# A hybrid flow step on one core: order of the output pairs' loads, spread-out weight sums and squares, and a last pair in pieces

## The chip, the cores and the metric

The kernel runs on one NeuronCore of a Trainium2 chip. Its engines are TensorE (PE in the profile; its weight loads are PEld), VectorE (DVE), ScalarE (ACT), GpSimd (POOL) and SyncE (SP), which here only issues DMAs. Each engine works through its own list of instructions in order and waits where an instruction needs something that another engine or a DMA has not finished. The metric is the time of one execution on the device, in microseconds. Before the change three runs took 2201.45, 2194.2 and 2185.36 us, so the median is 2194.2 us.

## What is computed

The reference is one layer of a backbone for 128 prompt tokens and 2048 sample tokens with 1024 channels. Both groups go through the same steps, which make 2176 token rows in all:

```python
xn = rmsnorm(h, ln_g) * (1.0 + scale) + shift
proj = einsum('btd,de->bte', xn, w_in)           # 1024 -> 7696 columns
o_a = delta_bidir(...)                            # gated DeltaNet scan, forward and backward
o_b = chunk_sgu(...);  o_c = fourier_mix(...)     # spatial gating, Fourier mixing
br = stack([o_a, o_b, o_c])                       # each 512 wide, times its SiLU gate
pb = einsum('btnw,nwd->btnd', br, w_branch)
merged = einsum('btnd,btnd->btd', sigmoid(gates), pb)
h = h + gate * einsum('btd,de->bte', merged, w_out)
y = rmsnorm(h, final_g)
```

The change touches the part from `pb` on: the merge of the three branches, the product with `w_out` and the last norm.

## The kernel before

Every fp32 product is made from float16 halves: each operand is written as a high and a low half (`halves`, or `converting` for weights: ACT writes the scaled high half, DVE the rest), and a product is three matmuls (high·high, high·low, low·high). The scale of the halves comes from a sum of squares, which ACT makes with an accumulating Square.

The work stands in stages. After the input projections, the DeltaNet scan runs piece by piece beside the spatial gating, the Fourier mixing and the first two merges (`pace.tick` starts the next piece). `merge(n, ...)` is called for the branches 1, 2 and 0 in this order. Each call goes over 8 blocks of 128 output channels (`db`), and in each over five tiles of tokens, four of 512 and one of 128. For a tile TensorE makes the gate's product (24 matmuls, or 8 x 3) and the branch's (12, or 4 x 3) into two of the three banks of PSUM named `ps_mm`; ACT makes the sigmoid of the first (L1711), DVE multiplies the second with it (L1720), POOL adds the result to the running sum `mrow` (L1721). A bank comes free when ACT or DVE has read it, so TensorE can be ahead of them by about one tile.

Beside this main line, other work is put in:

- In `merge(2)`, `finish_delta` (called at the start of each block) loads a block of the third branch's weights and sums its squares on ACT (L1764 to L1766), eight in all.
- In `merge(0)`, `tail` calls `out_w(db)` for the first four blocks. It prepares two of the eight column blocks of `w_out`: loads, two squares (L1803), two high and two low halves of 1024 elements (L1792 and L1793, called at L1810), and then four differences of weight quarters, made on POOL (L1814), split into halves and written to DRAM (`tD`).
- In `merge(0)` from the fifth block on, `quarters` makes from two blocks of merged values seven operands for a tile (sums and differences on DVE and POOL, then halves of 512, 256 and 1024 elements a partition) and writes them to DRAM (`paD`, L1833).
- `gate_rows` makes the adaLN gate in steps (L464 and L466 on DVE).

The output stage is `one_tile(16)` for the 128 prompt rows, then eight pairs of 128-row tiles. A pair takes seven products of 12 matmuls 512 wide in place of eight (Strassen's scheme on the 2 x 2 blocks of rows and of `w_out`): `two_tiles`. It needs the operands of the pair from DRAM (`next_pair`, L1896: 128 partitions x 14 KB, 1792 KB), the summed weights `tw` (L1906: four loads of 1 MB into the place of `xl`), the gate row `gb` (L1901) and the last norm's row `fg` (L1907), each 512 KB.

The operands lie in three buffers. One is in the pool `orp`; as `desk` the same bytes are the work place of `out_w` and `quarters` until the last L1833 has read them. Two are in the pool `op`, which opens in the place of `big` (`mrow` and the branch values `o16`) once `merge(0)` is over. Here pairs 0, 3 and 6 are loaded into the `orp` buffer, the others into `op`.

No list of times fixes the order. The kernel's scheduler orders the instructions of each engine, and so the DMAs on SP's queue, from the order of the source, from `high_priority` blocks and from `issue_after`, which puts an instruction behind a named one.

## Time and profile before

| | us |
|---|---|
| median of three runs | 2194.2 |
| the profiled execution, by its own clock of time | 2185.07 |
| its span from first to last instruction | 2183.3 |
| TensorE busy in the span | 2086.8 (96%) |
| VectorE, ScalarE, GpSimd busy | 1357.1, 1056.4, 765.5 |
| DMA moved | 403.36 MB, 185 GB/s on average |

The profiled execution was the fastest of the four that were timed; 1.8 us of its time lie outside the span. In a row of the profile, the number before the engine is the start or the busy time; the square bracket behind a row gives how long the engine stood idle before it and what ended the wait. The columns of a table by windows are busy time by engine with the number of instructions, then the clock that TensorE was granted (1.00 is full speed), the busy share of the DMA engines and what they moved.

### The profile page before, as it was taken

What the parts mean: (1) busy time and instruction counts of PE and PEld (TensorE: products, weight loads), DVE (VectorE), ACT (ScalarE), POOL (GpSimd) and SP (SyncE); (2) the same over time, 40 slices, a digit from 0 to 9 for tenths busy, and PEclk for the clock granted to TensorE, in tenths of its full rate; (3) what the DMA queues carried; (4) which work ended last, traced back from release to release, by engine and by line L of the source; (5) the groups of instructions that cost most, each with busy time, mean ns of one, the idle gap of its engine ahead of it and who ended that gap; (6) DMA issues with size and microseconds to landing.
All of it is one profiled execution on the core that took longest, in us unless ns stands there. A gap on an engine that the chain in (4) does not pass through costs nothing. (4 is left out here: it accounts for less than half of the span.)

```text
span 2183.3 us, 42589 instructions
## 1 busy us (share of the span) xinstructions
PE 2086.8 (96%) x16122; PEld 1193.9 (55%) x16122; DVE 1357.1 (62%) x3070; ACT 1056.4 (48%) x2428; POOL 765.5 (35%) x939
## 2 busy tenths in 40 slices
PE   7999999999899999999899999899999999997997
PEld 4455444465455677786555655456555444443443
DVE  6657754389879797466655546655564665565244
ACT  5544744466555664444644446655553433343111
POOL 0321432233434332444122223344533244334355
PEclk9999999999999999999999999999999999999999
DMA  9526631277776743444755456866654644457562
GB/s 351 217 71 203 250 125 71 95 239 217 240 231 210 234 140 95 128 142 129 225 165 167 153 170 205 255 203 200 209 187 152 203 161 166 161 186 295 193 236 111
DMA packets 222925, 403.36 MB, mean 185 GB/s; under 512 B 39720, under 2 KB 109888, under 8 KB 219904
## 3 DMA queue, kind: packets, MB, share of 16 engines
q1 hardware_dynamic: 167648, 290.98, 41.8%
q0 software_dynamic: 15248, 65.95, 8.3%
q10 hardware_dynamic: 39824, 43.72, 6.0%
q8 instruction: 126, 2.06, 0.4%
q14 instruction: 79, 0.65, 0.1%
HBM read 258.26 MB, written 142.30 MB: 183 GB/s over the span
## 5 line engine op out<-in xcount | busy, mean ns | idle before, releaser
L241 PE MATMUL b<-xh,whi 128*128 128x512 f16 (+1 forms) x1920 | 650.9, 348 | 8.4 <-DVE sg L1720 5.5
L241 PE MATMUL b<-xl,whi 128*128 128x512 f16 (+1 forms) x1920 | 651.1, 348 | 0.0
L241 PE MATMUL b<-xh,wlo 128*128 128x512 f16 (+1 forms) x1920 | 650.3, 348 | 0.0
L241 PEld LDWEIGHTS <-whi 128*128 128x128 f16 x3872 | 353.0, 98 | 329.9 <-issue 14.5
L241 PEld LDWEIGHTS <-wlo 128*128 128x128 f16 x1936 | 189.4, 98 | 176.4 <-issue 2.1
L241 PE MATMUL b<-big,bhi 128*128 128x512 f16 (+1 forms) x960 | 250.8, 348 | 3.8 <-ACT big L1677 2.6
L241 PE MATMUL b<-big,blo 128*128 128x512 f16 (+1 forms) x480 | 163.1, 347 | 0.2 <-DVE blo L318 0.2
L1721 POOL TENSOR_TENSOR mrow<-mrow,sg 128x512 f32<-128x512 f32 (+1 forms) x80 | 99.2, 1242 | 153.0 <-DVE sg L1720 119.3
L241 PEld LDWEIGHTS <-xh 128*128 128x128 f16 x1496 | 119.4, 99 | 32.5 <-issue 3.2
L943 POOL TENSOR_TENSOR cy<-cy,raw 128x545 f32<-128x545 f32 (+1 forms) x48 | 65.9, 1399 | 182.9 <-ACT raw L942 182.9
L241 PEld LDWEIGHTS <-bhi 128*128 128x128 f16 x960 | 86.1, 98 | 79.3 <-issue 4.0
L241 PEld LDWEIGHTS <-pa 128*128 128x128 f16 x684 | 66.9, 99 | 98.3 <-issue 20.7
L1711 ACT ACTIVATE sg<-b,winv 128x512 f32<-128x512 f32 (+1 forms) x120 | 73.8, 615 | 65.2 <-PE b L241 64.6
L241 PE MATMUL b<-whi,xh 128*128 128x128 f16 x544 | 96.1, 223 | 2.7 <-DVE yT L1629 1.9
L241 PE MATMUL b<-whi,xl 128*128 128x128 f16 x544 | 96.1, 223 | 0.0
L241 PE MATMUL b<-wlo,xh 128*128 128x128 f16 x544 | 96.1, 223 | 0.0
L1177 POOL COPY T<-ES 32x256 f16<-32x256 f16 x68 | 27.5, 404 | 191.6 <-DMA ES<-ei 172.8
L1720 DVE SCALAR_TENSOR_TENSOR sg<-b,binv,sg 128x512 f32<-128x512 f32 (+1 forms) x80 | 53.2, 666 | 62.1 <-PE b L241 55.4
L318 DVE SCALAR_TENSOR_TENSOR wlo<-wst,wsc,whi 128x1024 f16<-128x1024 f32 x52 | 68.9, 1327 | 33.3 <-ACT whi L317 33.3
L305 ACT ACTIVATE wlo<-wst 128x1024 f16<-128x1024 f32 x52 | 55.0, 1058 | 70.1 <-DMA wst<-in_w_blk_dram 65.2
L241 PE MATMUL b<-xl,pa 128*128 128x512 f16 x384 | 86.7, 379 | 1.6 <-DVE st L1967 1.6
L241 PEld LDWEIGHTS <-xl 128*128 128x128 f16 x816 | 74.6, 99 | 13.4
(506 smaller groups left out, 4256.2 us busy)
## 6 DMA issues: line engine op xcount, KB each, us to landing
wst<-in_w_blk_dram SPq DMA_DIRECT2D x58, 512.0 KB, 4.9
pa<-pa POOLq DMA_DIRECT2D x16, 896.0 KB, 4.1
pa<-pa SPq DMA_DIRECT2D x8, 1792.0 KB, 8.0
qkv<-cy POOLq DMA_DIRECT2D x12, 1089.0 KB, 5.3
st<-br SPq DMA_DIRECT2D x48, 256.0 KB, 3.6
mrow<-mrg SPq DMA_DIRECT2D x16, 576.0 KB, 3.9
dc<-dec SPq DMA_DIRECT2D x17, 512.0 KB, 4.2
kq<-qkv SPq DMA_DIRECT2D x34, 256.0 KB, 4.8
```

Of the source, the lines that this page charges most:

```text
L241: newest[0] = PE.matmul(out, l, r, start=start, stop=stop, skip_group_check=reopened)
L305: w.squared = A.activation(w.lo, st, AF.Square, accum_out=ss)
L318: w.low = V.scalar_tensor_tensor(w.lo, st, s, w.hi, ALU.mult, ALU.subtract)
L943: G.tensor_tensor(y[:, c0:c1], y[:, c0:c1], raw[:, 1 + c0:1 + c1], ALU.mult)
L1177: G.tensor_copy(T16[rows(a0, b), :, :, b], ES[0:32, :, 2 * a0 + b, :, wT])
L1711: A.activation(sg, ps, AF.Sigmoid, scale=gw.inv)
L1720: V.scalar_tensor_tensor(sg, ps, binv[:, 1:2], sg, ALU.mult, ALU.mult)
L1721: G.tensor_tensor(mr, mr, sg, ALU.add)
```

## The change

1. **Pairs' buffers and loads.** Pairs 2 and 5 now use the buffer in `orp`; pairs 0, 1, 3, 4, 6 and 7 use those in `op`. In the source the first pair's load stands behind the loads of `tw` 1 and 2, ahead of `gb`, of `tw` 0 and 3 and of `fg`.
2. **Squares of the third branch's weights.** They leave `finish_delta`; `norm_step` makes one after each tile from the third block of `merge(2)` on, behind that tile's sigmoid.
3. **`out_w` in steps.** It becomes a generator. `merge` calls `out_step` after each tile, which takes two steps. The halves of 1024 elements become two of 512, and each square stands behind a sigmoid.
4. **`quarters`.** The last halves, 1024 elements a partition, become two of 512.
5. **The last pair.** Its end goes by pieces for both tiles, as the last part of the diff shows.

```diff
     def finish_delta(db):
-        st = sb(ep, [P, 512], "st", bufs=3)
-        SY.dma_start(st, w_brb[0, db])
-        A.activation(st, st, AF.Square, accum_out=bsums[:, 3 + db:4 + db])
         if db == KT - 1:
             pace.drain()
+    early = list(range(KT))
+    def norm_step(db):
+        if db > 1 and early:
+            i = early.pop(0)
+            st = sb(ep, [P, 512], "st", bufs=3)
+            SY.dma_start(st, w_brb[0, i])
+            with tc.issue_after(gated_[0].ins):
+                A.activation(st, st, AF.Square, accum_out=bsums[:, 3 + i:4 + i])
-    inv_ = merge(2, False, inv_, finish_delta, then=(0, 17))
+    inv_ = merge(2, False, inv_, finish_delta, then=(0, 17), step=norm_step)
...
         for i in range(2):
-            halves(whi[:, :, cols_[i]], wlo[:, :, cols_[i]], sts[i], s)
+            for q in q4:
+                halves(whi[:, q, cols_[i]], wlo[:, q, cols_[i]], sts[i][:, q], s)
+            yield
...
+    def out_step(db):
+        nonlocal weights_out
+        for _ in range(2):
+            next(weights_out, None)
...
-        halves(T7[:, :, 0, 3:7], T7[:, :, 1, 3:7], S, ms_s)
+        for a in range(2):
+            halves(T7[:, a, 0, 3:7], T7[:, a, 1, 3:7], S[:, a], ms_s)
...
     def next_pair():
...
-            ready.append(operands(op, 2) if i % 3 else operands(orp, 1))
+            ready.append(operands(orp, 1) if i % 3 == 2 else operands(op, 2))
...
+    summed_in(1, 2)
+    next_pair()
     gb = sb(op, [P, D], "gb", bufs=1)
     fg = sb(op, [P, D], "fg", bufs=1)
     SY.dma_start(gb, gateD[0:1, :].to_broadcast([P, D]))
+    summed_in(0, 3)
+    SY.dma_start(fg, final_g[None, :].to_broadcast([P, D]))
-    next_pair()
-    for q in (1, 2, 0, 3):
-        SY.dma_start(tw[:, q].rearrange("p j l k c -> p j (l k c)"), tD[q])
-    SY.dma_start(fg, final_g[None, :].to_broadcast([P, D]))
...
+        total(u2, X, u2)
+        gated(1, right)
+        V.tensor_tensor(u2, u2, gb[:, right], ALU.mult)
         G.tensor_tensor(u2, u2, xr[0][:, right], ALU.add)
+        G.tensor_tensor(p1, p1, gb[:, left], ALU.mult)
+        G.tensor_tensor(p1, p1, xr[1][:, left], ALU.add)
+        product(Y, pa, 2, summed(3), False)
...
+        with tc.high_priority():
+            V.tensor_tensor(hh[1][:, left], Y, gb[:, left], ALU.mult)
+            sooner = V.tensor_tensor(hh[1][:, left], hh[1][:, left], p1, ALU.add)
+            piece(1, 1, left, V)
+        for i, cs, Z in ((1, slice(512, 896), bank(ps_mm, [P, 384])), (2, slice(896, D), bank(ps_mm, [P, P]))):
+            product(Z, pa, 6, quarter(4, cs.start, cs.stop - cs.start), True)
...
+        A.activation(hf[1], hf[1], AF.Copy, scale=norms[:, 1:2])
+        A.dma_start(y_sample[0, (t + 1) * P:(t + 2) * P], hf[1])
         out = y_sample[0, t * P:(t + 1) * P]
+        for cs in (slice(0, 640), slice(640, D)):
+            V.tensor_scalar(hf[0][:, cs], hf[0][:, cs], norms[:, 0:1], None, ALU.mult)
+            SY.dma_start(out[:, cs], hf[0][:, cs])
```

Three places show how the order of instructions moves. The first is SP's queue at the passage from `merge(0)` to the output stage, behind the last load of `tw`. `xh` are rows of `x` for the residual; `out_dram` is the prompt's output. Before, `pa_25660` and `pa_25662` are the operands of pairs 1 and 2 and `pa_25650` those of pair 0:

```order
L1906 DMA xl_95<-tw 128x4096 x2
L1901 DMA gb_25644<-gate 128x1024
L1907 DMA fg_25645<-in_final_g_dram 128x1024
L1896 DMA pa_25660<-pa 128x4x1792
L1896 DMA pa_25662<-pa 128x4x1792
L1914 DMA xh_94<-in_x_sample_dram 128x1024
L1922 DMA out_dram<-xh_94 128x1024
L1896 DMA pa_25650<-pa 128x4x1792
```

After the change `pa_25694`, `pa_25707` and `pa_25709` are the operands of the pairs 0, 1 and 2:

```order
L1930 DMA xl_95<-tw 128x4096 x2
L1926 DMA pa_25694<-pa 128x4x1792
L1936 DMA gb_25696<-gate 128x1024
L1938 DMA fg_25697<-in_final_g_dram 128x1024
L1926 DMA pa_25707<-pa 128x4x1792
L1947 DMA xh_94<-in_x_sample_dram 128x1024
L1955 DMA out_dram<-xh_94 128x1024
L1926 DMA pa_25709<-pa 128x4x1792
```

Pair 0's load has moved from behind the store of the prompt's output to the head, ahead of `gb` and `fg`; the four loads of `tw` stay ahead of it, and pair 2's load now stands behind the store. On TensorE the first pair's products were those of pair 1 for 36 matmuls, then came pair 0's; after the change pair 0's are first.

The second place is ACT at the start of `merge(2)`, where scan pieces run beside it (the names `o`, `oss`, `S`, `Q`, `R` and `kn` are the scan's). Before:

```order
L1766 ACTIVATE st_19364,bsums_93<-st_19364 128x512
L1192 ACTIVATE R_1306_10912<-b_18719 32x4x32
L305 ACTIVATE blo_19264,bsums_93<-wst_18959 128x512
L1192 ACTIVATE R_1306_10912<-b_18719 32x4x32
L1766 ACTIVATE st_20036,bsums_93<-st_20036 128x512
L1766 ACTIVATE st_20713,bsums_93<-st_20713 128x512
L1286 CAST kn_2207_18847<-skn_18797 128x512
L1766 ACTIVATE st_21396,bsums_93<-st_21396 128x512
L1372 ACTIVATE of_18734,oss_429_3918<-o_18497 128x512
L1766 ACTIVATE st_22082,bsums_93<-st_22082 128x512
L1207 ACTIVATE Q_10514<-b_18870 64x256
L1220 ACTIVATE S_2195_18771<-S_16870 128x512
```

After, the same stretch has no squares:

```order
L1192 ACTIVATE R_1306_10912<-b_18716 32x4x32
L305 ACTIVATE blo_19261,bsums_93<-wst_18956 128x512
L1192 ACTIVATE R_1306_10912<-b_18716 32x4x32
L1286 CAST kn_2206_18844<-skn_18794 128x512
L1372 ACTIVATE of_18731,oss_429_3918<-o_18497 128x512
L1207 ACTIVATE Q_10514<-b_18867 64x256
```

They stand further back instead, each behind the sigmoid (L1713) of one of the eight tiles from the third block on, two of them here:

```order
L1713 ACTIVATE sg_20279<-b_20186,winv_19643 128x512
L1779 ACTIVATE st_20326,bsums_93<-st_20326 128x512
L1192 ACTIVATE T_1273_10506<-b_20315 32x4x32
L1220 ACTIVATE u_20306<-sv_20095 128x512
L1192 ACTIVATE R_1272_10504<-b_20315 32x4x32
L317 ACTIVATE whi_20182<-wst_20012,wsc_20335 128x1024
L1362 ACTIVATE of_20351,oss_20354<-o_20193 128x128 x4
L1192 ACTIVATE R_1272_10504<-b_20315 32x4x32
L1713 ACTIVATE sg_20426<-b_20344,winv_19643 128x512
L1779 ACTIVATE st_20491,bsums_93<-st_20491 128x512
```

The third place is DVE in the first block of `merge(0)`, between the products with the sigmoid. Before, all of the first `out_w`'s halves (`wolo` and `pa`) stand ahead of the first and the second tile's L1720:

```order
L1757 TENSOR_TENSOR st_23246<-b_23248,st_23246 2x256
L1793 SCALAR_TENSOR_TENSOR wolo_23185<-pa_23189,wsc_23218,wohi_23184 128x8x128 x2
L1793 SCALAR_TENSOR_TENSOR pa_23189<-sums_23190,wsc_23218,pa_23189 128x512 x2
L1720 SCALAR_TENSOR_TENSOR sg_23281<-b_23283,binv_23206,sg_23281 128x512
L1793 SCALAR_TENSOR_TENSOR pa_23189<-sums_23190,wsc_23218,pa_23189 128x512 x2
L1720 SCALAR_TENSOR_TENSOR sg_23327<-b_23329,binv_23206,sg_23327 128x512
```

After, these two (now L1722) stand free, and the halves, in smaller pieces mixed with `gate_rows` (L464, L466), stand ahead of the third tile's, which is 128 wide:

```order
L1822 COPY winv_2754_23186<-wsc_23318 128x1 x2
L315 TENSOR_TENSOR winv_23342<-wsc_23338,xsc_382 128x1
L464 TENSOR_SCALAR sg_23220<-wst_23221,scT_103 128x256 x2
L466 SCALAR_TENSOR_TENSOR sg_23220<-wst_23221,scT_103,sg_23220 128x256
L1804 SCALAR_TENSOR_TENSOR wolo_23185<-pa_23189,wsc_23318,wohi_23184 128x4x128
L466 SCALAR_TENSOR_TENSOR sg_23220<-wst_23221,scT_103,sg_23220 128x256 x2
L1804 SCALAR_TENSOR_TENSOR wolo_23185<-pa_23189,wsc_23318,wohi_23184 128x4x128 x2
L466 SCALAR_TENSOR_TENSOR sg_23220<-wst_23221,scT_103,sg_23220 128x256
L1804 SCALAR_TENSOR_TENSOR wolo_23185<-pa_23189,wsc_23318,wohi_23184 128x4x128
L466 SCALAR_TENSOR_TENSOR sg_23220<-wst_23221,scT_103,sg_23220 128x256
L1804 SCALAR_TENSOR_TENSOR pa_23189<-sums_23190,wsc_23318,pa_23189 128x512
L1722 SCALAR_TENSOR_TENSOR sg_23369<-b_23371,binv_23206,sg_23369 128x128
```

The two `wolo` halves of 1024 elements have become four of 512. Of the eight pieces that an `out_w` has now, five stand with the gate's sums ahead of the 128-wide tile's L1722, and the other three behind it; before, four of six stood ahead of the first tile's L1720 and two ahead of the second's. The rows for the third block read the same; in the second and fourth the gate's sums stand elsewhere.

More of the change, by code (lines that the diff above doesn't have):

```diff
@@ L1678, in branch_block, with merge @@
             V.scalar_tensor_tensor(o16[:, 1, g, t0:t0 + tn], st, s, o16[:, 0, g, t0:t0 + tn], ALU.mult, ALU.subtract)
-    def merge(n, first, inv, each=None, halves=HALVES, mid=None, then=None):
+    gated_ = [None]
+    def merge(n, first, inv, each=None, halves=HALVES, mid=None, then=None, step=None):
         steps, sinv = iter(()), None
@@ L1875, in tail @@
     def tail(db):
+        nonlocal weights_out
+        if db < 5:
+            for _ in weights_out:
+                pass
         if db < 4:
-            out_w(db)
+            weights_out = out_w(db)
+            next(weights_out)
         if db == KT - 1:
@@ L1976, in two_tiles @@
             V.tensor_tensor(hh[0][:, left], a, gb[:, left], ALU.mult)
-        (V if end else G).tensor_tensor(hh[0][:, left], hh[0][:, left], xr[0][:, left], ALU.add)
+        G.tensor_tensor(hh[0][:, left], hh[0][:, left], xr[0][:, left], ALU.add)
         product(Y, pa, 5, summed(2), False)
@@ new lines, in two_tiles @@
+        for i, cs, Z in ((1, slice(512, 896), bank(ps_mm, [P, 384])), (2, slice(896, D), bank(ps_mm, [P, P]))):
+            product(Z, pa, 6, quarter(4, cs.start, cs.stop - cs.start), True)
+            with tc.high_priority(), tc.issue_after(sooner.ins):
+                V.tensor_tensor(hh[0][:, cs], Z, gb[:, cs], ALU.mult)
+                V.tensor_tensor(hh[0][:, cs], hh[0][:, cs], u2[:, cs.start - 512:cs.stop - 512], ALU.add)
+                piece(0, i, cs, V if i == 2 else G)
+        summed_up(1, 1)
```

70 lines of the change are left out of this document (38 added, 32 removed).

## The prediction

> **What bounds the kernel now.** I read the page first (busy time of the engines), then the list of what TensorE waited for, and then the stretches in which the long ones lie.
>
> ```profile
> PE 2086.8 (96%) x16122; PEld 1193.9 (55%) x16122; DVE 1357.1 (62%) x3070; ACT 1056.4 (48%) x2428; POOL 765.5 (35%) x939
> ...
> PE b L241 <- DMA pa<-pa: 14.4, 2, 14.1
> PE b L241 <- ACT S L1220: 7.3, 6, 2.2
> PE b L241 <- DVE sg L1720: 5.5, 5, 1.8
> PE b L1369 <- ACT o L1365: 4.8, 2, 3.4
> ...
> PE b L241 <- DVE st L1967: 1.6, 1, 1.6
> ...
> PE b L241 <- DVE xh L2003: 0.6, 1, 0.6
> ```
>
> TensorE is busy 96% of the span and no other engine over 62%. The change takes no matmul out, so it can gain only from TensorE's 96 us of idle time, and from the few microseconds behind its last matmul. The columns of a wait are its total, how often, and the longest. One wait stands out, 14.1 us for the operands of the first pair.
>
> **The passage to the output stage.** These rows of the timeline, in order of time, show that wait: start, length, engine, and in brackets the idle time before.
>
> ```profile
> 1995.54 1.20 SPq L1906 DMA_DIRECT2D xl<-tw  x2
> 2004.49 0.42 DVE L1829 TENSOR_TENSOR sums<-mrow,sums 128x256 f32<-128x256 f32 x1
> 2005.05 0.32 SPq L1901 DMA_DIRECT2D gb<-gate  x1
> 2005.43 0.44 SPq L1907 DMA_DIRECT2D fg<-in_final_g_dram  x1
> 2006.03 1.07 SPq L1896 DMA_DIRECT2D pa<-pa  x2
> 2008.30 0.38 PE L241 MATMUL b<-wolo,whi 128*128 128x512 f16 x1
> 2008.52 0.38 PE L241 MATMUL b<-wohi,wlo 128*128 128x512 f16 x1
> 2016.56 1.90 POOL L1860 TENSOR_TENSOR gb<-gb,winv 128x1024 f32<-128x1024 f32 x1 [3.36 <-DMA gb<-gate]
> 2017.80 1.74 DVE L1921 SCALAR_TENSOR_TENSOR xh<-xh,hss,fg 128x1024 f32<-128x1024 f32 x1 [5.40 <-DMA fg<-in_final_g_dram]
> 2020.10 0.37 SPq L1896 DMA_DIRECT2D pa<-pa  x1
> 2023.03 0.58 PE L241 MATMUL b<-wohi,pa 128*128 128x512 f16 x1 [14.13 <-DMA pa<-pa]
> 2033.79 0.39 PE L241 MATMUL b<-wohi,pa 128*128 128x512 f16 x1 [0.28 <-DMA pa<-pa]
> ```
>
> The loads land in the order in which SP issued them: `gb` at 2016.56, `fg` at 2017.80, the first pair's operands at 2023.03. So 0.5 MB cost 1.24 us, and the 1.8 MB of a pair 5.23 us. At 2005.05, when `gb` is issued, the queue still holds the summed weights. It is rid of them 1.24 us before `gb` is in, at about 2015.3. The windows say that the DMA engines are full all the time:
>
> ```profile
> 2008.00:2012.00 4.00, 0.90 (x5) 0.19 (x2) 0.71 (x2) 0.94 (x1) 2.00 (x2) 0.90 1.01 426
> 2012.00:2016.00 4.00, 0.00 (x0) 0.00 (x0) 0.15 (x1) 0.21 (x2) 0.57 (x1) 0.50 1.01 418
> ...
> 2024.00:2028.00 4.00, 4.00 (x11) 1.32 (x9) 0.00 (x0) 0.00 (x0) 0.00 (x0) 0.50 1.03 409
> 2028.00:2032.00 4.00, 4.00 (x19) 1.81 (x18) 0.00 (x0) 0.00 (x0) 0.00 (x0) 0.97 1.02 411
> ```
>
> The last three columns are the clock granted to TensorE, the DMA engines' busy share and GB/s. The share is 1.0 up to 2032: this wait is bytes, not latency.
>
> After the change pair 0's load takes the place of `gb` at the head. It needs the bytes of `mrow`, which DVE reads last at 2004.49, as `gb` does now, so it is issued at about 2005.05 too. What it overtakes is `gb` and `fg`, 2 x 1.24 = 2.5 us; the weights stay ahead of it. It lands at 2015.3 + 5.23 = 2020.5, **2.5 us earlier**. The second wait, 0.28 us, goes as well, since the next operands needed are pair 1's, issued straight behind `fg` and needed 60 matmuls later. What is late next: `fg` lands at about 2023.0, and DVE's L1921 waits for it, with the first pair's totals queued behind it on DVE; it ends at about 2024.8. The first product of 12 matmuls ends later than that, since 11 of them take 4 us at the half clock of these rows. `gb`, with its 1.90 us on POOL, is ready at about 2023.7, before the first pair multiplies by it. Pair 2's load now stands behind the prompt's store and has a pair's time to land. Term: **-2.8**, bounds 0 and -3.3 (the 5.23 us were 4.4 at the 410 GB/s of these windows).
>
> The clock is the second cost of this gap: it is 0.50 until about 2028. At full speed matmuls follow each other by 0.22 us (2008.30 and 2008.52); 11 of them in the 4 us from 2024 lose 4 - 11 x 0.22 = 1.6 us, and the microsecond from 2023.03 on as much in proportion and the first of the next window the rest, about 2.5 us in all. A gap of 11.6 us leaves this as it is. [...]
>
> **The start of the second merge, 1395 to 1431.**
>
> ```profile
> 1400.00:1450.00 50.00, 44.26 (x395) 26.40 (x393) 27.88 (x74) 30.83 (x90) 24.20 (x34) 0.97 0.69 219
> 1450.00:1500.00 50.00, 50.00 (x461) 30.36 (x459) 28.78 (x75) 26.48 (x77) 24.57 (x30) 1.00 0.69 209
> ...
> L1766 ACT ACTIVATE st<-st 128x512 f32<-128x512 f32 x8 | 5.0, 627 | 3.5 <-DMA st<-in_w_brb_dram 3.5
> L1766 ACT ACTIVATION_READ_ACCUMULATOR st<-st 128x1 f32 x8 | 1.5, 187 | 0.0
> ...
> 1409.35 0.63 ACT L1766 ACTIVATE st<-st 128x512 f32<-128x512 f32 x1 [1.17 <-DMA st<-in_w_brb_dram]
> 1410.53 0.20 PE L241 MATMUL b<-R,Q 128*128 128x64 f16 x1 [1.48 <-ACT Q L1207]
> 1423.08 0.45 SPq L282 DMA_DIRECT2D wst<-in_w_blk_dram  x1
> 1428.23 1.06 ACT L305 ACTIVATE wlo<-wst 128x1024 f16<-128x1024 f32 x1 [3.88 <-DMA wst<-in_w_blk_dram]
> ```
>
> In these 50 us TensorE idles 5.7, in the next 50 not at all. The eight squares take ACT 5.0 + 1.5 us and 3.5 more waiting for their loads, 10 us together among the scan's pieces. One of them stands 1.17 us for its load, the scan's `Q` comes late behind it, and TensorE waits 1.48. The longest wait in the list for L1369 (3.4) is of another kind: ACT stands 3.88 us for `wst`, whose load SP issued only at 1423.08, behind another load that waits for the scan, and the scan's `o` stands behind it on ACT. After the change no square stands there, and in SP's order this load comes ahead of the other. I count the 1.48 in full and 2.5 of the 3.4: **-4.0**, bounds 0 (the scan's own chain is the limit) and -5.7 (all idle time of the window). The squares now come one a tile in the third and fourth block, 8 x (0.63 + 0.19) = 6.5 us of ACT. The cover is ACT's idle time, 23.5 us in the quoted window of 50. TensorE has none there, so a square that stands in front of something due shows at once; I take 1 in 8 of this time, **+0.8**, bounds 0 and 6.5.
>
> **The last merge.** TensorE waits five times for L1720, 5.5 us.
>
> ```profile
> L466 DVE SCALAR_TENSOR_TENSOR sg<-wst,scT,sg 128x256 f32<-128x256 f32 x38 | 21.5, 608 | 1.9 <-DMA wst<-in_w_ada_dram 1.9
> ...
> L1793 DVE SCALAR_TENSOR_TENSOR pa<-mrow,msc,pa 128x512 f16<-128x512 f32 x16 | 12.1, 758 | 0.0
> ...
> L1793 DVE SCALAR_TENSOR_TENSOR wolo<-pa,wsc,wohi 128x1024 f16<-128x1024 f32 x8 | 9.9, 1278 | 0.5 <-ACT wohi L1792 0.5
> ...
> 1739.29 3.94 DVE L1793 SCALAR_TENSOR_TENSOR pa<-sums,wsc,pa 128x512 f16<-128x512 f32 x2 [1.60 <-ACT pa L1792]
> 1743.95 0.38 PE L241 MATMUL b<-xh,whi 128*128 128x512 f16 x1 [1.76 <-DVE sg L1720]
> 1746.54 2.71 DVE L464 TENSOR_SCALAR sg<-wst,scT 128x256 f32<-128x256 f32 x2
> ```
>
> The largest, 1.76, follows two of `out_w`'s halves that took 3.94 us in place of about 1.5 and stood ahead of L1720. In the new order these pieces stand ahead of the 128-wide tile's product instead, and with them the gate's sums: 2.71 + 5 x 0.61 + 5 x 0.76 = 9.6 us of DVE in one run. What it may take: from the end of the tile before, TensorE can do the 128-wide tile (36 matmuls of a quarter of 0.22, 2.0 us) and one more tile (36 x 0.22 = 7.9 us) before it needs that bank, 9.9 us, of which L1720 itself takes about 1.0 before and behind the run. So I expect a new wait of about 1 to 2 us in the first and third block, where the order has this run, and none in the others. The old five go but for one or two at the quarters: 5.5 - 1.0 - 2 x 1.5 = **-1.5**, bounds -5.5 (all go) and +3.5 (the old five stay and a 1.76 comes twice more).
>
> A split costs DVE 2 x 0.758 - 1.278 = 0.24 us by these rows, 24 splits (8 of `wolo`, 16 of `quarters`) 5.8 us in the stage's 330, which its idle time hides outside such a run. [...]
>
> **The last pair.**
>
> ```profile
> 2167.64 0.69 DVE L1967 TENSOR_TENSOR xh<-b,st 128x512 f32<-128x512 f32 x1
> ...
> 2173.56 0.22 PE L241 MATMUL b<-wohi,pa 128*128 128x128 f16 x1
> ...
> 2178.56 0.34 SPq L2016 DMA_DIRECT2D out_dram<-xh  x1
> ```
>
> TensorE's two waits here are the 1.6 and 0.6 of the list. The 384-wide product gets a bank of its own and fills the first; the 128-wide one has its own too, so the second goes: TensorE ends up to 2.2 us earlier than 2173.78. Behind its last matmul the chain to the last store's issue takes 4.8 us now. After the change DVE does multiply, add and multiply by `fg` for the other tile's left half, 3 x 0.69, where one 0.69 stood, so 1.4 of the 2.2 go back: **-0.8**, bounds -2.2 and +0.6 (two more such steps fall on the chain).
>
> **Sum:** -2.8 - 4.0 + 0.8 - 1.5 - 0.8 = -8.3 us. On the profiled execution, 2185.07 (span 2183.3), this gives 2176.8. That execution is 9 us below the median of the three runs, 2194.2, so the time on the scale of the median is 2185.9, rounded 2186. The three runs lie 0.7% apart; a change of under 1% is about what cannot be told from none here.
>
> **The rivals.**
> - *The whole gap goes* (0.06). If the weights had landed when pair 0's load is issued, 14.1 + 0.3 + 2.5 of clock go in place of 2.8: 14.1 us more, 2171.8. Against it: a DMA share of 1.0 from 2008 on, and the weights stay ahead in SP's order.
> - *The waits only move* (0.27). L1720's waits come back at the 128-wide tile and the scan's chain limits 1395 to 1431; passage and last pair remain, -3.6, so 2190.6. For it: the run of 9.6 us against 9.9 - 1.0.
> - *The load is not earlier* (0.10). If the queue shared its rate among the loads instead of serving them in turn, pair 0's would land with `gb` and `fg` as now; -5.5, so 2188.7. Against it: the 1.24 us between `gb` and `fg`.
> - *Slower: the squares stop ACT* (0.10). In the third and fourth block TensorE has no idle time. If every square waits for its load as at 1409.35, it holds ACT 1.17 + 0.63 + 0.19 = 2.0 us, 16 us for eight. All else gains 9.1, so the kernel is 7 us slower, 2201. It turns slower from 1.14 us a square. Against it: 1410.53 is the only place where a square was seen to hold TensorE, and three loads fit into their buffers ahead.
>
> **How the numbers follow.** My forecast has 0.47. The range 2172 to 2200 takes in the second and third rival and most of the fourth's and first's cases. It covers the sum of the bounds and the 5 to 8 us by which single runs differ. Faster by over 1% needs the first rival or nearly all upper bounds: 0.07. Slower by over 1%, 22 us, needs the fourth with `out_w`'s bound on top: 0.05. Within 1%: 0.88.
>
> **What the new profile would show.** The first pair's matmul at about 2020 on the old scale, with a wait of 11 to 12 us and half clock behind it; no idle time on ACT for the squares' loads, and the window after 1400 over 48 busy; waits for L1722 of 1 to 2 us at two 128-wide tiles; the last matmul some 2 us earlier against the last store, which gains less. A passage without a wait, or waits in the third and fourth block of the second merge, would prove me wrong.

## The result: 0.6% faster, inside the range, with one term of the wrong sign

Over ten runs each, the changed kernel takes 2178.7 us (median) and the one before 2193.3 us. The ratio is 0.9938, with a 95% interval of 0.9915 to 0.9961: some 14 us faster, with 9 to 19 us in the interval. The forecast was a gain of 8.3 us and a range of 2172 to 2200 us, in which 2178.7 lies. The gain stays under 1%, to which the prediction gave 0.88.

The profiled executions differ by less than the medians: the span falls from 2183.3 to 2174.7 us, 8.6 us. The execution of before that was profiled is one of the fastest of its kernel (2185.07 against a median of 2193), so the medians give the size of the gain and the traces show where it lies.

The list of what TensorE waited for, after:

```profile
PE 2085.2 (96%) x16122; PEld 1191.9 (55%) x16122; DVE 1368.0 (63%) x3099; ACT 1061.8 (49%) x2454; POOL 761.9 (35%) x939
...
PE b L241 <- DMA pa<-pa: 3.5, 1, 3.5
...
PE b L241 <- ACT sg L1713: 2.9, 2, 1.7
...
PE b L241 <- DVE wlo L1804: 2.6, 1, 2.6
...
PE b L1369 <- ACT o L1365: 1.7, 2, 1.3
...
PE b L241 <- DVE blo L318: 1.4, 2, 1.2
...
PE b L241 <- DVE sg L1722: 1.3, 1, 1.3
```

The wait for the first pair's operands is 3.5 us in place of 14.1. L1369 fell from 4.8 to 1.7, the gated product (L1722, before L1720) from 5.5 to 1.3. Three kinds are new or longer: for the sigmoid itself (L1713), for `wlo`, the low half of the prompt tile's operands, and for `blo` (L318, 1.2 us at 1831.86, in the last merge). In the last merge TensorE's waits come to 5.3 us (2.85 + 1.22 + 1.26), against 5.5 before: they moved more than they shrank.

To place the gain, I cut each trace at the same work: the start of the 41st sigmoid of the three merges (the first of `merge(2)`), the 71st, the 119th, the first pair's first matmul, and the span's end. Before, these stand at 1398.5, 1662.0, 1988.3, 2023.0 and 2183.3 us. The stretches, in us:

| | second merge | last merge | passage | output stage |
|---|---|---|---|---|
| before | 263.5 | 326.3 | 34.7 | 160.3 |
| after | 260.2 | 325.9 | 29.7 | 160.0 |
| after, a second profile | 262.9 | 324.8 | 30.9 | 161.1 |

"Last merge" begins some tiles before `merge(0)` does. The start of the second merge differs by up to 10 us between profiles of kernels that are the same up to there (1396.5 to 1406.4), which is why single stretches and not whole spans are compared below.

**The passage after**, in rows of the timeline (start, length, engine, and in brackets the idle time before):

```profile
1992.18 1.06 SPq L1930 DMA_DIRECT2D xl<-tw  x2
1996.24 3.58 DVE L1804 SCALAR_TENSOR_TENSOR wlo<-wst,msc,whi 128x1024 f16<-128x1024 f32 x1
1996.71 2.03 POOL L1885 TENSOR_TENSOR sg<-sg,inv 128x512 f32<-128x512 f32 x2
1999.88 0.39 PE L241 MATMUL b<-wohi,wlo 128*128 128x512 f16 x1 [2.58 <-DVE wlo L1804]
2003.87 0.37 SPq L1926 DMA_DIRECT2D pa<-pa  x1
2004.29 0.50 SPq L1936 DMA_DIRECT2D gb<-gate  x1
2009.88 0.75 POOL L1858 DMA_DIRECT2D pa<-pa  x1 [0.84 <-DVE pa L1804]
2014.72 0.59 PE L241 MATMUL b<-wohi,pa 128*128 128x512 f16 x1 [3.48 <-DMA pa<-pa]
2017.88 1.90 POOL L1885 TENSOR_TENSOR gb<-gb,winv 128x1024 f32<-128x1024 f32 x1 [2.34 <-DMA gb<-gate]
```

Pair 0's load is issued at 2003.87 and TensorE starts on it at 2014.72, 10.85 us later, ahead of `gb`. New is the DVE row: the low half takes 3.58 us beside POOL's work, and the prompt tile's product waits 2.58 us for it. So the prompt tile ends later than before (2011.24, 26.2 us after the cut, against 20.6), and part of the old gap is now in front of it. The new wait has its own price in clock, as the window behind it shows: TensorE works all of these 4 us at a mean granted clock of 0.62, and behind the second wait it is 0.83 and 0.75 in the windows from 2012 and 2016.

```profile
2000.00:2004.00 4.00, 4.00 (x13) 1.50 (x12) 2.33 (x5) 0.89 (x2) 1.27 (x1) 0.62 1.00 411
```

**The start of the second merge, and the last merge, after**: three rows of the table by windows (the five engines' busy time, the clock, the DMA share, GB/s), then rows of the timeline:

```profile
1400.00:1450.00 50.00, 49.12 (x449) 29.69 (x448) 30.50 (x82) 28.90 (x82) 26.31 (x35) 1.00 0.69 215
1450.00:1500.00 50.00, 49.02 (x444) 29.30 (x442) 26.97 (x73) 28.23 (x82) 22.32 (x28) 1.00 0.71 216
1500.00:1550.00 50.00, 48.97 (x444) 29.47 (x443) 29.95 (x82) 31.21 (x95) 24.48 (x32) 1.00 0.70 215
...
1417.24 0.35 SPq L282 DMA_DIRECT2D wst<-in_w_blk_dram  x1
...
1771.67 0.63 ACT L305 ACTIVATE blo<-wst 128x512 f16<-128x512 f32 x1 [8.76 <-DMA wst<-in_w_brb_dram]
1772.30 0.67 ACT L1713 ACTIVATE sg<-b,winv 128x512 f32<-128x512 f32 x1
1773.02 0.27 PE L241 MATMUL b<-big,bhi 128*128 128x128 f16 x2 [1.15 <-ACT sg L1713]
```

TensorE is busy 49.1 of the 50 us from 1400 on, against 44.3; in each of the next two windows it loses 1 us that it did not lose before. The squares now lie between 1488 and 1552, but neither loss stands behind one: the first is a wait of 0.98 us at 1471.56, ahead of them, and the second a wait of 1.03 us at 1544.03 for `o` (L1230), before which ACT had stood idle 3.73 us until a DMA. The load of `wst` is issued at 1417.24 in place of 1423.08. In the last merge the new wait for the sigmoid is no matter of DVE: ACT stands 8.76 us on L305 for the next block's weights to arrive, and the sigmoid is queued behind that.

**The end, after**, from the timeline:

```profile
2157.98 2.75 PE L241 MATMUL b<-xl,pa 128*128 128x512 f16 x12
...
2161.34 0.22 PE L241 MATMUL b<-wohi,pa 128*128 128x128 f16 x1
...
2162.24 0.15 DVE L2038 TENSOR_SCALAR part<-part 128x1 f32<-128x1 f32 x1 [1.92 <-ACT xh L2030]
2162.31 0.68 DVE L2052 TENSOR_TENSOR xh<-b,gb 128x512 f32<-128x512 f32 x1
2163.09 1.35 DVE L2053 TENSOR_TENSOR xh<-xh,sg 128x512 f32<-128x512 f32 x1
...
2169.44 0.81 SPq L2072 DMA_DIRECT2D out_dram<-xh  x2
```

TensorE's last matmul comes 12.2 us earlier than before (2161.34 against 2173.56), but SP's last two stores are issued only from 2169.44 on, the first 8.1 us behind it and the second 8.5, where the last store was 5.0 behind. DVE has a hand in this that the first and third row show: the other tile's product, which L2052 multiplies, is done at 2160.73, but DVE stands idle for 1.92 us, until 2162.24, because a sum for the norm (L2038) is ahead of L2052 in its list and waits for a square on ACT. Seven of the eight profiles with the new end (all but e11) have this idle time, 1.91 or 1.92 us.

### The profile page after: what moved, and what is told of

Same layout as the page of the kernel before. It is cut to its first block, busy times and chain, and to the rows that moved or that the text cites. A ratio compares the mean times of both kernels' runs of the same rounds, so it can differ in the third digit from the quotient of the medians.

```text
span 2174.7 us, 42636 instructions
## 1 busy us (share of the span) xinstructions
PE 2085.2 (96%) x16122; PEld 1191.9 (55%) x16122; DVE 1368.0 (63%) x3099; ACT 1061.8 (49%) x2454; POOL 761.9 (35%) x939
## 5 line engine op out<-in xcount | busy, mean ns | idle before, releaser
L1723 POOL TENSOR_TENSOR mrow<-mrow,sg 128x512 f32<-128x512 f32 (+1 forms) x80 | 92.2, 1153 | 146.9 <-DVE sg L1722 113.1
L1713 ACT ACTIVATE sg<-b,winv 128x512 f32<-128x512 f32 (+1 forms) x120 | 73.9, 616 | 66.1 <-PE b L241 65.3
L1722 DVE SCALAR_TENSOR_TENSOR sg<-b,binv,sg 128x512 f32<-128x512 f32 (+1 forms) x80 | 53.3, 666 | 63.1 <-PE b L241 58.3
L318 DVE SCALAR_TENSOR_TENSOR wlo<-wst,wsc,whi 128x1024 f16<-128x1024 f32 x52 | 72.6, 1397 | 28.3 <-ACT whi L317 28.2
L305 ACT ACTIVATE wlo<-wst 128x1024 f16<-128x1024 f32 x52 | 55.0, 1058 | 68.2 <-DMA wst<-in_w_blk_dram 62.6
L1284 POOL TENSOR_TENSOR skn<-skn,ed 128x512 f32<-128x512 f32 x34 | 38.7, 1138 | 122.6 <-DMA skn<-kv 118.7
```

Of the source, the lines that this page charges most:

```text
L305: w.squared = A.activation(w.lo, st, AF.Square, accum_out=ss)
L318: w.low = V.scalar_tensor_tensor(w.lo, st, s, w.hi, ALU.mult, ALU.subtract)
L1284: G.tensor_tensor(h3(kn_), h3(kn_), bc(ed[:, d, t, :], P), ALU.mult)
L1713: gated_[0] = A.activation(sg, ps, AF.Sigmoid, scale=gw.inv)
L1722: V.scalar_tensor_tensor(sg, ps, binv[:, 1:2], sg, ALU.mult, ALU.mult)
L1723: G.tensor_tensor(mr, mr, sg, ALU.add)
```

## Experiments

Each kernel is the changed one with an edit; its ratio is to the kernel before, on the same chip. The table gives the four stretches of each profile. None of these intervals lies clear of the changed kernel's (0.9915 to 0.9961), so the ratios alone settle no single part; the stretches and the waits in the traces have to.

| | second merge | last merge | passage | output stage | ratio (95%) |
|---|---|---|---|---|---|
| e1 part 1 undone | 259.9 | 328.0 | 34.2 | 161.1 | 0.9956 (0.9939 to 0.9972) |
| e2 part 2 undone | 268.2 | 323.8 | 31.3 | 161.1 | 0.9966 (0.9945 to 0.9988) |
| e3 parts 3, 4 undone | 259.4 | 329.4 | 31.6 | 160.7 | 0.9957 (0.9936 to 0.9977) |
| e4 part 5 undone | 258.9 | 323.9 | 28.9 | 157.4 | 0.9904 (0.9867 to 0.9941) |
| e5 weights behind | 259.3 | 324.2 | 25.3 | 160.3 | 0.9919 (0.9890 to 0.9947) |
| e6 = e5, old end | 258.5 | 325.1 | 25.6 | 159.4 | 0.9895 (0.9875 to 0.9916) |
| e7 scaling behind | 257.6 | 328.7 | 31.2 | 160.2 | 0.9937 (0.9913 to 0.9961) |
| e8 = e6 and e7 | 260.1 | 326.2 | 29.4 | 157.8 | 0.9914 (0.9892 to 0.9935) |
| e9 = e8, store late | 259.5 | 326.4 | 25.8 | 160.5 | 0.9928 (0.9907 to 0.9950) |
| e10 = e6, store late | 260.9 | 326.9 | 25.5 | 160.0 | 0.9918 (0.9889 to 0.9946) |
| e11 store late alone | 258.2 | 324.4 | 29.5 | 161.2 | 0.9928 (0.9905 to 0.9951) |
| e12 changed, again | 262.9 | 324.8 | 30.9 | 161.1 | 0.9931 (0.9908 to 0.9953) |

### e1: the loads as before

```diff
-            ready.append(operands(orp, 1) if i % 3 == 2 else operands(op, 2))
+            ready.append(operands(op, 2) if i % 3 else operands(orp, 1))
...
-    summed_in(1, 2)
-    next_pair()
...
+    next_pair()
+    summed_in(1, 2, 0, 3)
```

> The changed kernel with part 1 alone undone: buffers and loads of the pairs as before (pair 0 in the orp buffer, its load behind the prompt's store; gb and fg ahead). My theory (the passage is bytes in issue order): of the 12.2 us by which TensorE's last matmul came earlier, about 6.8 lie at the passage; undone, the first pair's matmul waits 11 to 14 us for its load again, and the kernel is 5 to 7 us slower than the changed one. Rival (the gain there came from the earlier loads of the summed weights, which the other parts bring): the wait falls from 14.1 us by 3 or more without part 1, and the kernel loses at most 2.5 us.

In e1 the two waits for the pairs' loads in the timeline are:

```profile
2020.41 0.58 PE L241 MATMUL b<-wohi,pa 128*128 128x512 f16 x1 [9.04 <-DMA pa<-pa]
2031.05 0.39 PE L241 MATMUL b<-wohi,pa 128*128 128x512 f16 x1 [0.97 <-DMA pa<-pa]
```

The passage is 34.2 us again, as before (34.7); the five profiles with part 1 and nothing else moved there (after, e2, e3, e4, e12) have 28.9 to 31.6, on average 30.5. The wait is 9.0 us, where 11 to 14 were expected, and so fell by more than the 3 us that the rival named; it is shorter than the 14.1 of before because the prompt tile ends later (25.2 us after the cut, against 20.6), not because the load came sooner. Part 1 is worth about 4 us here, and 0.3 to 1 us at the second wait. By the ratios e1 is some 4 us slower than the changed kernel, less than the 5 to 7 expected. The rival with the earlier weights falls on the passage: without part 1, next to nothing of its gain is left.

### e2: the squares as before

```diff
     def finish_delta(db):
+        st = sb(ep, [P, 512], "st", bufs=3)
+        SY.dma_start(st, w_brb[0, db])
+        A.activation(st, st, AF.Square, accum_out=bsums[:, 3 + db:4 + db])
...
-    inv_ = merge(2, False, inv_, finish_delta, then=(0, 17), step=norm_step)
+    inv_ = merge(2, False, inv_, finish_delta, then=(0, 17))
```

> The changed kernel with part 2 alone undone: the eight squares and their loads again at the start of the second merge. My theory (the squares and the late load behind them held ACT): the 44th gate's sigmoid comes 5 to 6 us later again against the one three tiles before, TensorE waits 3 to 5 us more in 1400 to 1431, and 2 us of this are given back by the 57th tile, where the squares now stand; in sum 3 to 4 us slower than the changed kernel. Rival (the scan's own chain sets that stretch and the two profiles differ by chance): the stretch keeps the gain, within 1 us.

What TensorE waited for in e2 between 1396 and 1540, the four largest:

```profile
PE b L1369 <- ACT o L1365: 3.0, 1, 3.0
PE b L241 <- ACT S L1220: 2.0, 3, 1.0
PE b L241 <- DVE S L1221: 1.7, 2, 1.2
PE b L241 <- ACT Q L1207: 1.3, 1, 1.3
```

The waits for `o` and `Q` of before are back, in the same size. The second merge takes 268.2 us, and 263.5 before; in the ten other kernels' profiles that have part 2, and in the changed kernel's two, it takes 257.6 to 262.9, on average about 260. That is 4 to 8 us. Cut finer, the gain is clearest in the merge's first block (from its first sigmoid to the next block's), where the squares stood: 49.6 us before and 49.2 in e2, 42.5 to 44.4 in the twelve profiles with part 2, with TensorE idle for 5.7 and 5.4 us against 0.0 to 1.6. The rival (chance) falls there. Of the rest of e2's 268.2, its third block has a part that neither before nor any other profile has: two waits of 2.0 us together from 1524 on, and a granted clock of 0.74 and 0.83 in the windows behind. Part 2 has a price further on: in the fourth block TensorE idles 0.5 to 2.1 us in each of the twelve profiles with it, and not at all in the two without. So some 4 us of the whole stretch are part 2's, near the 3 to 4 expected. How much of this is the squares on ACT and how much the load of `wst` was not separated.

### e3: the preparation of the weights as before

```diff
-            weights_out = out_w(db)
-            next(weights_out)
+            for _ in out_w(db):
+                pass
...
-            for q in q4:
-                halves(whi[:, q, cols_[i]], wlo[:, q, cols_[i]], sts[i][:, q], s)
+            halves(whi[:, :, cols_[i]], wlo[:, :, cols_[i]], sts[i], s)
...
-        for a in range(2):
-            halves(T7[:, a, 0, 3:7], T7[:, a, 1, 3:7], S[:, a], ms_s)
+        halves(T7[:, :, 0, 3:7], T7[:, :, 1, 3:7], S, ms_s)
```

> The changed kernel with parts 3 and 4 alone undone: out_w in one piece as before, halves of 1024, and the loads of the summed weights kept ahead of pair 0's. My theory: the finer steps gain next to nothing in the last merge (0.2 us in the profile), so from the first to the last sigmoid of that merge the kernel is within 1.5 us of the changed one; the waits for the gated product are about 5 us again, and the new waits for ACT's sigmoid and for DVE's halves go. Rival (the steps gain what the list of waits says): 4 us slower there.

In the last merge of e3, TensorE waits for one thing alone:

```profile
PE b L241 <- DVE sg L1722: 7.3, 5, 2.4
```

The five waits of before are back. The stretch takes 329.4 us, and 326.3 before; the profiles with the steps have 323.8 to 328.7, on average 325.7. The two without them are on average some 2 us longer, but the one of before lies inside the others' scatter. So a gain of the steps is not shown; the figures lie between the theory and its rival. In e3 the prompt tile's low half held nobody up, and the passage was no shorter for it (31.6).

### e4: the last pair as before

The edit puts back the end of `two_tiles` (the lines with a minus in that part of the change).

> The changed kernel with part 5 alone undone: the last pair's end as before. My theory (TensorE ends 2.3 us earlier, but DVE's chain behind it is 3.5 us longer): TensorE's last matmul comes about 2.3 us later, the last store is issued about 4.8 us after it in place of 8.3, and the kernel is 1 us faster than the changed one. Rival (the new end gains, as it was meant to): 1 to 2 us slower.

The last matmul and the last store of SP in e4:

```profile
2155.74 0.22 PE L241 MATMUL b<-wohi,pa 128*128 128x128 f16 x1
...
2161.11 0.34 SPq L2050 DMA_DIRECT2D out_dram<-xh  x1
```

They are 5.4 us apart, against 8.5 to the last store of the changed kernel. The output stage takes 157.4 us; in eight profiles with the new end it takes 160.0 to 161.2. Here the old end is the better one by about 3 us, and e4 is the second fastest kernel of the study by its ratio, though its interval (0.9867 to 0.9941) overlaps the changed one's. That is more than I expected, for a reason that the profile shows: of TensorE's two waits in the old end, the 1.6 us for L1967 is not there in e4, nor in e6 and e8; in the profile of before DVE came late to L1967, behind two 1024-wide products of which one took 2.29 us in place of 1.28. The wait can come back with the old end: e9 and e10, below, have it. In e4 only the 0.6 us remain to be gained by a bank of its own, and the chain on DVE costs more. So the old end takes 157.4 to 159.4 us where this wait stays away, and 160.0 to 160.5 where it is there (before, e9, e10), about as much as the new end.

### e5, e6: weights behind

```diff
-    summed_in(0, 3)
-    SY.dma_start(fg, final_g[None, :].to_broadcast([P, D]))
+    ahead = SY.dma_start(fg, final_g[None, :].to_broadcast([P, D]))
+    with tc.issue_after(ahead.ins):
+        summed_in(0, 3)
```

> The changed kernel with two of the four loads of summed weights (2 MB, needed only by a pair's fifth and sixth product) moved behind the first pair's operands, gb and fg on SP's queue. My theory (the passage is bytes in issue order): 2 MB at 410 GB/s are 4.9 us, so the wait for the first pair's load, 2.2 to 6.3 us in the kernels with part 1, goes, and the time from the last-but-one sigmoid of the last merge to the first pair's matmul falls from 29 to 31 us to about 26.5, where the prompt tile's own end limits it; with the full clock kept this is 3 to 5 us faster than the changed kernel. Rival (the queue shares its rate, or the next load is late instead): the wait goes on to pair 1's operands or to the summed weights, and nothing is gained.

> The same with part 5 undone too (the last pair's end as before). My theory: from TensorE's last matmul to the issue of the last store 5.0 to 5.4 us in place of 8.0 to 8.1, from the first pair's matmul to TensorE's last about 2 us more; so some 1 us faster than the kernel before it in this list. Rival: the new end is the better one once TensorE runs without a gap, and this is 1 us slower.

The passage falls to 25.3 and 25.6 us, and the first pair is not waited for in e5 (0.4 us in e6): 2 MB fewer ahead of it are worth about 5 us, as expected. One part of the rival holds too: the second pair's operands, now behind 2 MB, are waited for 2.2 us in e5 and 2.0 in e6, so that 3 us of the 5 remain. By its ratio e5 is some 4 us below the changed kernel, as expected, but the intervals overlap. The old end saves 0.9 us of the output stage in e6. By its ratio e6 is the fastest kernel here, 0.9895, with an interval (0.9875 to 0.9916) that just overlaps those of the changed one (0.9915 to 0.9961 and 0.9908 to 0.9953).

### e7, e8: POOL's scaling behind the low half

```diff
-            V.tensor_scalar(inv8, winv, pre[0][1], None, ALU.mult)
+            with tc.issue_after(pre[0][2].ins):
+                V.tensor_scalar(inv8, winv, pre[0][1], None, ALU.mult)
```

(`single` now also returns the instruction that writes the low half.)

> The changed kernel with POOL's scaling of the prompt's gate row made to wait until DVE has written the low half of the prompt's operands (the instruction that took 3.58 us beside it, and 1.28 before). My theory (DVE is held up while POOL works in SBUF beside it, but the load sets the passage): that low half takes about 1.3 us, TensorE's wait of 2.6 us for it goes, and the wait for the first pair's load grows by the same, so that the time from the last-but-one sigmoid to the first pair's matmul stays at 29 to 31 us and the kernel is within 1 us. Rival: the time falls by 2.6 us.

> All three: two loads of weights behind, the old end of the last pair, POOL's scaling behind the low half. My theory: with the load out of the way the 2.6 us count, so the time from the last-but-one sigmoid to the first pair's matmul falls to about 24 us, and this is the fastest kernel, 5 to 8 us below the changed one. Rival: it is no faster than without the third part.

The collision was understood rightly: with POOL out of the way the low half took 1.59 us in e7 and 1.60 in e8 in place of 3.58, and TensorE's wait for it fell to 0.6 us. In e7 the passage stayed, as expected: the 2 us came back as a wait for the load. But in e8 it rose, to 29.4 us from e6's 25.6, where about 24 were expected, and e8 is not the fastest kernel, as I had expected, but behind e6. The rows of e8, and one window of it:

```profile
2001.60 0.39 PE L241 MATMUL b<-wohi,wlo 128*128 128x512 f16 x1 [0.59 <-DVE wlo L1804]
...
2007.12 0.38 SPq L1927 DMA_DIRECT2D pa<-pa  x1
...
2010.93 0.75 POOL L1858 DMA_DIRECT2D pa<-pa  x1
...
2018.66 0.58 PE L241 MATMUL b<-wohi,pa 128*128 128x512 f16 x1 [7.40 <-DMA pa<-pa]
...
2014.00:2016.00 2.00, 0.00 (x0) 0.00 (x0) 0.15 (x1) 0.57 (x2) 0.57 (x1) 1.00 0.94 189
```

The load takes 11.5 us from its issue, against 7.8 in e6. What differs in the order of events is the last store of `quarters` (L1858, 0.9 MB): with DVE freer it is issued 3.8 us after the load, in e6 6.0 us after it. My theory did not have this store in it. The store's own bytes are not what held the load up, though: from 2008.5 to 2016.0 GpSimd's queue moved 0.00 MB and SP's 2.17. What the trace shows is that the DMA engines slowed: from 2014 to 2016 they were busy for 94% of the time but moved only 189 GB/s.

### e9, e10, e11: the last store late

```diff
+        if k == 3 and t0 == 512:
+            held.append(write)
+        else:
+            write()
...
         two_tiles(t, ready[i], *rows_, i == 7)
+        if held:
+            with tc.issue_after(gated_[0].ins):
+                held.pop()()
+            next_pair()
         next_pair()
```

> The store late as well, with two loads of weights behind, the old end of the last pair and POOL's scaling behind the low half. My theory: without the store the load lands 6 to 8 us after its issue, as in the kernels where only the weights were put behind (7.8 or less), and TensorE waits 1 to 4 us for it, so the first pair's matmul comes about 25 us after the last-but-one sigmoid; without the wait for the low half it would be 23. Rival (it was not the store that made the load late when POOL's scaling was moved): 29 us again.

> The store late, two loads of weights behind, the old end of the last pair; POOL's scaling as in the changed kernel, so that TensorE waits 2.6 us for the low half. My theory: no wait for the first pair's load nor for the second pair's (2.0 us without the late store), first pair's matmul about 25.5 us after the last-but-one sigmoid; 4 to 8 us below the changed kernel in time. Rival: pair 2's load, which now stands behind the store, is late, and TensorE waits there instead.

> The changed kernel with one thing more: the last store of quarters (0.9 MB, rows that only the seventh pair reads) is issued behind the first pair's work on POOL in place of some 3 to 7 us after the first pair's load; pair 2's load, which needs its buffer, comes behind it. In the six kernels run with part 1, the load takes 10.7 to 14.7 us from issue to landing, and the longer the sooner that store is issued after it. My theory (store and load share the DMA engines, and the store's 0.9 MB are 2.2 us): the load lands 8 to 10.5 us after its issue, and the time from the last-but-one sigmoid to the first pair's matmul is at most 29 us. Rival (only the loads ahead on the same queue count): it stays at 10.7 us or more.

With the store away, in e9, the first pair's matmul comes 7.8 us after the issue of its load, in place of 11.5, the passage is 25.8 us in place of 29.4, and the window from 2014 to 2016 has 395 GB/s. So the slow stretch went with the store, in one profile of each; that the store made it is not shown, for its bytes had not begun to move, and in e2, e3, e7 and e12 a store issued 3.3 to 5.7 us after the load left the DMA engines at 421 to 423 GB/s.

In e10 the first pair's matmul comes 7.4 us after the issue, and the second pair is no longer waited for; but TensorE still waits 1.7 us for the first, where no wait was expected, and by its ratio e10 is 3 us below e12, not 4 to 8, with overlapping intervals.

e11 missed: 11.9 us from issue to matmul, not 8 to 10.5, and so on the side of its rival (only the same queue counts). Set beside the kernels that have the weights ahead too, the time from the load's issue to the first pair's matmul was 14.7 us in e3 (store 3.3 us after the load), 13.8 in e7 (3.8), 13.0 in e12 (4.3), 13.4 in e2 (5.7), 10.9 after (6.0), 10.7 in e4 (7.2) and 11.9 in e11 (no store). What each queue moved between issue and matmul explains this list. `q1` is SP's queue, `q0` GpSimd's, and the two pairs of rows are the changed kernel's (2003.87 to 2014.72) and e11's (2005.83 to 2017.71):

```profile
q1 hardware_dynamic: 932, 4.32, 95.9%
q0 software_dynamic: 41, 0.26, 5.7%
...
q1 hardware_dynamic: 1090, 4.93, 100.1%
q0 software_dynamic: 27, 0.08, 1.6%
```

The second number is MB. e11 had no store in its way, but 0.6 MB more of its own queue, more of the weights being still on the way when the load was issued. In e2, e3, e7 and e12 GpSimd's queue moved 0.9 to 1.3 MB in this time and SP's 4.6 to 4.9. In all seven the two together moved at 421 to 423 GB/s: here both queues count, and 0.9 MB of a store are 2.2 us (an estimate from these figures). A store 6 us behind the load came too late to share.

e9 and e10 give the gain back in the output stage (160.5 and 160.0 us: the wait for L1967's counterpart is there again, 2.5 and 2.6 us), and neither beats e6 by its ratio.

### e12: the changed kernel again

> The changed kernel itself once more, beside these three on the same chip. Expected: ratio to the kernel before 0.992 to 0.996 again, the first pair's matmul 28.5 to 31.5 us after the last-but-one sigmoid, from TensorE's last matmul to the issue of the last store about 8 us; the profiles of one kernel differ by several us ahead of the last two merges, which no part of the change touches.

The ratio, 0.9931, agrees with the first. Its profile shows the 2.6 us for `wlo` again, and 7.4 us for the first pair's load where the first profile had 3.5: with its store at 4.3 us behind the load, not 6.0, the passage is 30.9 us.

## Why the prediction was right, term by term

The time lay in the range and the sign was right; the gain was 14 us (9 to 19) against 8.3 forecast. Two mechanisms, the passage and the start of the second merge, are borne out; that the sum came so near is in part luck, since it hides one term of the wrong sign and one that is not shown.

- **Passage, -2.8 forecast; -4 to -5 measured** (34.2 and 34.7 without part 1, 30.5 on average with it, and the second wait). The mechanism was right: bytes in issue order, the weights still ahead, a gap that stays, with a lowered clock behind it (0.83 and 0.75 in the windows from 2012 and 2016). The size was off in the landing: I took the 10.3 us ahead of the load at its issue for SP's queue alone. In the profile of before, 3.09 MB moved in this time on SP's queue and 1.27 MB on GpSimd's, stores that I had not counted, most of them of the last one, which was issued 3.3 us after the first of these loads (2008.31 against 2005.05). In the changed kernel it was issued 6.0 and 4.3 us after it, and 0.26 and 0.93 MB of stores shared the load's time. It came later because DVE was held up at `wlo`: a new wait of 2.6 us that I had not foreseen, and that the load hid. For the same reason the wait at the first pair was 3.5 and 7.4 us in the two profiles, not 11 to 12. That a shorter gap leaves the loss of clock as it is was an estimate: TensorE worked 5.2 us at half clock before (2023.03 to 2028.23), and after 3.3 us behind this wait (from 2014.72) and 3.4 behind the new one for `wlo` (from 2000.95). In e4, behind a gap of only 2.21 us, the clock was still at half for 3.41 us.
- **Start of the second merge, -4.0 + 0.8 forecast; about -4 measured** (263.5 against 260 on average with part 2). e2 brought back the very waits that the prediction named. The gain in 1400 to 1450 was 4.9 us of TensorE's time in the profile (44.26 to 49.12) against 4.0. Further back part 2 costs TensorE 0.5 to 2.1 us of waiting, against 0.8 forecast, but in the changed kernel's trace that wait stands behind a DMA and not behind a square.
- **Last merge, -1.5 forecast; 0 to -2 measured, not shown.** The stretch fell by 0.4 and 1.5 us, inside the scatter, and the waits in it from 5.5 to 5.3 us. The step that failed inside this term is the run of 9.6 us on DVE ahead of the 128-wide tile's product: I priced L464 at 2.71 us for two from a row of before in which DVE was held up. In the changed kernel the two took 0.61 us and the run 7.3 us in all (1738.1 to 1745.3), so no wait came in the first and third block. Waits of the forecast size came all the same, 1.2 and 1.7 us, elsewhere: at the sigmoids of the second and fourth block, behind loads that ACT stood for (8.76 and 10.76 us).
- **Last pair, -0.8 forecast; no gain, and up to +3.** The output stage took 160.0 to 161.2 us with the new end, 157.4 to 159.4 with the old one in e4, e6 and e8, and 160.0 to 160.5 with it before and in e9 and e10. Two steps failed. TensorE's 1.6 us before L1967 do not always come with the old end (e4, e6, e8 do not have them). And from the last matmul to the last store the chain grew by 3.1 to 3.5 us, not 1.4: I counted two more DVE steps of 0.69 us, but left out that DVE stands 1.92 us at L2038 ahead of them, 1.5 of it after their product is done, and that its steps could take longer than 0.69 (L2053 1.35 us).
- **The rivals.** The queue that shares its rate among its loads is ruled out: the load landed ahead of `gb`, as the order said (TensorE starts on it at 2014.72, POOL on `gb` at 2017.88), and e5's 2 MB were worth 5 us. But loads and stores of two queues did share (421 to 423 GB/s for both together), which that rival should have named. That the squares stop ACT, 16 us for eight, did not come true: what TensorE loses there is 2 us at most. The whole gap did not go: waits of 3.5 and 2.6 us are left. The waits only moved in the last merge, but not at the start of the second.

The four stretches add up to 784.8 us before, and to 775.8 and 779.7 in the changed kernel's two profiles: 9 and 5 us gained, where the medians say 14 with 9 to 19. The rest is not placed: there is one profile of before, 8 us below the median, and the part ahead of the second merge, which no part of the change touches, differs by up to 10 us between profiles.

## What to carry to other kernels

When a queue is full, work out the start of a consumer from the bytes ahead of its load, and count every queue, stores too: here 2 MB of the same queue were worth 5 us, and 0.9 MB of a store from another engine about 2 (the estimate from 421 to 423 GB/s). A wait that stands ahead of a longer one on the same path is no gain until the longer one goes (e7). At the end of a kernel, count the instructions of the engine that finishes, not of the one that was waiting: two saved waits of TensorE were bought with 3 us more behind its last matmul.

## What the runs showed of the hardware

- One instruction of DVE, the low half of 128x1024 (`wlo`), took 3.58 us beside POOL's L1885 in all nine profiles that have the two together (after, e1, e2, e4, e5, e6, e10, e11, e12), 1.59 or 1.60 us once L1885 was made to wait (e7, e8, e9), and 1.28 us before and in e3; 3.58 is 2.8 times 1.28. Not every work of POOL did this: before, an addition of POOL (1998.60 on) ran beside the last 0.56 us of those 1.28.
- The granted clock fell after a gap of 2.21 us in e4 and stayed at 1.00 over one of 2.17 us in e5. In e4 TensorE waited 2.21 us for the first pair, from 2006.03 to 2008.24, and ran at half clock from 2009.56 to 2012.97, for 3.41 us. Half clock lasted as long after, from 2000.95 to 2004.36 and from 2014.60 to 2018.01, and 17.07 us before, from 2011.16 to 2028.23. In windows of 3.41 us, e4:

```profile
2006.15:2009.56 3.41, 1.32 (x7) 0.64 (x8) 0.76 (x2) 1.15 (x2) 1.25 (x1) 1.00 1.05 433
2009.56:2012.97 3.41, 3.41 (x10) 1.21 (x9) 0.12 (x1) 0.59 (x1) 2.44 (x2) 0.50 0.99 411
```

In e5, a wait of 2.17 us for the second pair, from 2020.96 to 2023.13, cost no clock at all:

```profile
2018.39:2021.80 3.41, 2.57 (x12) 0.98 (x10) 0.92 (x2) 0.00 (x0) 0.00 (x0) 1.00 1.01 410
2021.80:2025.21 3.41, 2.08 (x10) 0.99 (x11) 0.47 (x1) 0.00 (x0) 2.53 (x2) 1.00 1.02 418
2025.21:2028.62 3.41, 3.41 (x18) 1.54 (x16) 0.00 (x0) 0.59 (x1) 0.00 (x0) 1.00 0.92 374
```

So two gaps of about 2.2 us ended differently. In these rows 2.09 us of e4's gap lie in the one window ahead of the drop, and e5's gap is split over two, 0.84 and 1.33; whether this made the difference is not shown.
